# Prompt attention of a hybrid decoder step: high and low parts of the values side by side as one matmul's weights

## The chip, the cores and the metric

The kernel runs on one core of one Trainium2 chip. The metric is the device time of one launch in microseconds (us), lower is better; the time of a kernel is the median of its runs. The engines of a core are TensorE (PE, matrix products; its weight loads are shown as PEld), VectorE (DVE), ScalarE (ACT), GpSimd (POOL) and SyncE (SP), which issues most transfers. Each engine takes its instructions in the order in which the program holds them, and an instruction that waits holds up those behind it on its engine.

## The reference

One layer is applied to a prompt of 512 tokens and to 8 sample sequences of 8 new tokens with 2048 cached positions each. A latent attention and a convolution module share an input projection; their normalised outputs are concatenated and projected, and a gated feed-forward network with a short convolution follows. The change lies in the attention of the prompt, for which the reference computes (cut):

```python
def mla_attend(q_lat, q_rope, kv, q_pos, k_pos):
    ...
    s = jnp.einsum('bthc,bsc->bhts', q_lat, ckv) + jnp.einsum('bthr,bsr->bhts', q_rope, kr)
    ...
    p = jax.nn.softmax(s, axis=-1).astype(ckv.dtype)
    return jnp.einsum('bhts,bsc->bthc', p, ckv)
...
    attn = jnp.einsum('bthc,chv->bthv', o_lat, w_uv).reshape(b, t, D_ATT)
    mixed = jnp.concatenate([rmsnorm(attn, g_attn_out), rmsnorm(conv_y, g_conv_out)], axis=-1)
    x = x + mixed @ w_o
```

There are 8 heads (H) with values of 64 columns each (DV); everything is in fp32. The kernel forms for the prompt the values v = ckv · w_uv of all heads first (NP = 512 tokens as 4 blocks of 128) and multiplies the probabilities of a head with them.

## The kernel before

**Products of pairs.** TensorE works here on a rounded fp32 type. To keep the precision, an operand is held as a pair: `split` (L109 to L111) copies it rounded on ScalarE (the high part, L110) and subtracts that from the original on VectorE (the low part, L111). `mm3` (L122 to L125) multiplies two pairs in three matmuls: high by high (L123), high by low (L124), low by high (L125).

**Stages.** In the profiled execution the input projection and the convolution's input run to about 110 us; the decode stage, attention of the sample sequences over the cached pages with the convolution between it, to about 320 us; the prompt's attention from then to some 437 us, with the output projection of the convolution's half (`proj_conv`) laced in; then the rest of the output projection and, from about 460 us, the feed-forward network.

**Decode.** `load_chunk` fetches pages of the cache through SP's queue into the tiles `CR`. For a sequence `bt`, `rope_rows_of` (L599 to L602) copies the rotary columns of its four chunks `CR` to `RP` on ScalarE; `rope_keys` transposes `RP` on TensorE (bank `krb`). `keys` transposes a chunk (bank `ktb`) and splits it into `kh` and `kl`, and `scores` (L637 to L640) multiplies them with the queries (bank `sb`).

**Prompt attention.** `values_of(k)` computes the values of 128 tokens for all heads into a bank and splits them into `vh` and `vl`. These tiles hold, for each block k and pair of heads, three slots of 64 columns: first head, zeros, second head. `open_right` sets the zeros with eight memsets (L844, L845). A head then goes through

- `keys_of` for a pair of heads (bank `kb`), `head_in`: queries and keys split into `qT` and `kT`;
- `score(h, j)` for row blocks j = 0 to 3 (L970 to L973, bank `spb`, two of them): columns of 128 (j + 1); VectorE takes the maximum (L975), ScalarE the exponential into a buffer of the ring `Pm` (L977, three buffers);
- `prob`, `prob_T`: normalised, transposed by TensorE (bank `tb`) and split into the pair `PTp` (called `PT` in the code);
- `attend(h, k)` (L1001 to L1008), the value product: for k = 0 to 3 one `mm3` with 512 − 128 k columns into the bank `pv`. The weights of the first head of a pair are its 64 values and the 64 zeros, those of the second head the zeros and its values, so that both heads of a pair add into one bank of 128 rows;
- for each pair of heads `head_out` (copy `raw` of the bank, L1012; scaled and split into `atph` and `atpl`, L1013, L1014) and `head_ss` (transposes of `raw` by TensorE into the bank `rawb`, and their squares).

**What sets the order.** The program is written as generators in which the front of head h + 1 alternates with the back of head h. A scheduler places each instruction of an engine by a priority, the place in the program plus an offset from the table `PR` (L146), which `prio(key)` adds. The tiles' memory is planned by a pool; a tile that takes memory which another one used waits for that one's last reader. The keys in question are `rr` (`rope_rows_of`), `cn` and `l1` (parts of the convolution's normalisation), `r0`, `pn` (parts of decode) and `kT` (the key's rotary rows of the prompt).

## Time and profile before

| what | us |
|---|---|
| median of 3 runs | 895.66 |
| lowest and highest run | 895.3 and 901.98 |
| the profiled execution's own time | 892.08 |
| its span (first to last recorded instruction) | 890.3 |

The profiled execution is another one than the three timed runs. A row of the trace names start and duration, the engine, the line of the kernel (for `split`, `mm3` and transposes that of the helper), what is written from what, partitions by elements, and in brackets the idle time ahead of the instruction with what ended it. The duration of a matmul reaches into the next one, since they are pipelined; the distance between two starts is what a matmul costs in a row of them. PEclk or granted clock is the share of TensorE's full clock (2.4 GHz) that was granted; 0.50 is its lower level of 1.2 GHz.

### The profile page before, as it was taken

What the parts mean: (1) busy time and instruction counts of PE and PEld (TensorE: products, weight loads), DVE (VectorE), ACT (ScalarE), POOL (GpSimd) and SP (SyncE); (2) the same over time, 40 slices, a digit from 0 to 9 for tenths busy, and PEclk for the clock granted to TensorE, in tenths of its full rate; (3) what the DMA queues carried; (4) which work ended last, traced back from release to release, by engine and by line L of the source; (5) the groups of instructions that cost most, each with busy time, mean ns of one, the idle gap of its engine ahead of it and who ended that gap; (6) DMA issues with size and microseconds to landing.
All of it is one profiled execution on the core that took longest, in us unless ns stands there. A gap on an engine that the chain in (4) does not pass through costs nothing.

```text
span 890.3 us, 16024 instructions
## 1 busy us (share of the span) xinstructions
PE 850.3 (96%) x5724; PEld 756.0 (85%) x5724; DVE 652.4 (73%) x1159; ACT 452.6 (51%) x1028; POOL 310.8 (35%) x402
## 2 busy tenths in 40 slices
PE   6999998899989999999989999999999999999995
PEld 5999887577656767877769999999999999999994
DVE  5277449779998777777666777985677998689664
ACT  6224735777767887456444443444333443333353
POOL 3020499999991020000102121440011331078143
PEclk9999989989999999999999999999999999999998
DMA  6223153454333004010343222223322223422512
GB/s 220 93 63 100 40 166 86 130 151 129 93 107 84 24 25 154 24 49 27 116 141 126 93 79 87 72 73 95 119 76 91 72 72 95 142 72 61 196 37 107
DMA packets 53828, 84.33 MB, mean 95 GB/s; under 512 B 6066, under 2 KB 39795, under 8 KB 53748
## 3 DMA queue, kind: packets, MB, share of 16 engines
q1 hardware_dynamic: 53458, 82.75, 30.0%
q8 instruction: 45, 0.74, 0.4%
q10 hardware_dynamic: 290, 0.56, 0.2%
q14 instruction: 35, 0.29, 0.1%
HBM read 76.95 MB, written 6.34 MB: 94 GB/s over the span
## 4 chain that ended last, share of the span: by engine, by line
PE 85%; DVE 5%; ACT 3%; SPq 3%; issue 2%; DMA 1%; POOL 1%; POOLq 0%; DVEq 0%; ACTq 0%
PE ub L133 11%; PE ub L131 11%; PE ub L129 10%; PE db L125 3%; PE db L123 3%; PE db L124 3%; PE ob L703 3%; PE gb L133 2%; PE wob L123 2%; PE wob L125 2%; PE wob L124 2%; PE gb L129 2%; PE ktb L107 2%; PE gb L131 2%; PE pq L123 1%
## 5 line engine op out<-in xcount | busy, mean ns | idle before, releaser
L133 PE MATMUL ub<-h2h,wup_l 128*128 128x288 f32 x704 | 153.1, 294 | 0.6 <-DVE wup_l L111 0.6
L131 PE MATMUL ub<-h2l,wup_h 128*128 128x288 f32 x704 | 152.9, 295 | 0.0
L129 PE MATMUL ub<-h2h,wup_h 128*128 128x288 f32 x704 | 152.1, 293 | 0.0
L133 PEld LDWEIGHTS ub<-h2h,wup_l 128*128 128x128 f32 x704 | 113.4, 188 | 0.9 <-DVE wup_l L111 0.8
L129 PEld LDWEIGHTS ub<-h2h,wup_h 128*128 128x128 f32 x704 | 113.5, 188 | 0.1
L131 PEld LDWEIGHTS ub<-h2l,wup_h 128*128 128x128 f32 x704 | 113.0, 187 | 0.0
L111 DVE TENSOR_TENSOR wup_l<-wup_r,wup_h 128x1024 fp32r<-128x1024 f32 x44 | 56.3, 1278 | 50.7 <-ACT wup_h L110 50.7
L249 POOL TENSOR_TENSOR acc<-acc,ct 128x512 f32<-128x512 f32 x65 | 91.4, 1406 | 5.4
L110 ACT CAST wup_h<-wup_r 128x1024 fp32r<-128x1024 f32 x44 | 46.3, 1052 | 89.4 <-issue 48.2
L119 POOL TENSOR_TENSOR rstd<-ms,mhalf 128x1 f32<-128x1 f32 (+3 forms) x25 | 16.6, 671 | 214.5 <-ACT junk L1023 111.0
L1251 POOL COPY nf<-U 128x2 f32<-128x2 f32 x44 | 23.1, 526 | 122.0 <-ACT U L1249 122.0
L248 POOL TENSOR_SCALAR ct<-gx,vc 128x512 f32<-128x512 f32 x65 | 62.1, 956 | 6.0
L1247 POOL COPY U<-sfs 128x16 f32<-128x16 f32 x44 | 19.7, 453 | 98.4 <-DVE uo L1258 90.4
L111 DVE TENSOR_TENSOR kl<-ktb,kh 128x512 fp32r<-128x512 f32 x64 | 42.4, 682 | 8.0 <-ACT kh L110 7.6
L107 PE MATMUL ktb<-ident,CR 128*128 128x128 f32 x256 | 44.0, 285 | 0.6 <-DVE kl L111 0.5
L1258 DVE SCALAR_TENSOR_TENSOR uo<-U,vc,uo 128x592 f32<-128x592 f32 x44 | 39.3, 893 | 1.4
L1257 DVE SCALAR_TENSOR_TENSOR uo<-U,vc,uo 128x592 f32<-128x592 f32 x44 | 39.2, 892 | 1.0
L110 ACT CAST kh<-ktb 128x512 fp32r<-128x512 f32 x64 | 35.9, 588 | 7.6 <-PE ktb L107 4.3
L107 PEld LDWEIGHTS ktb<-ident,CR 128*128 128x128 f32 x256 | 30.8, 143 | 8.3 <-issue 4.6
L703 PE MATMUL ob<-CR,PF 128*64 128x256 f32 x128 | 36.8, 396 | 0.0
L1256 DVE TENSOR_SCALAR uo<-U,vc 128x592 f32<-128x592 f32 x44 | 31.3, 712 | 0.1
L637 PE MATMUL sb<-kh,QL 128*128 128x512 f32 x64 | 29.1, 454 | 2.4 <-DVE mx L644 1.8
(422 smaller groups left out, 2453.1 us busy)
## 6 DMA issues: line engine op xcount, KB each, us to landing
wup_r<-in_wup_dram SPq DMA_DIRECT2D x44, 512.0 KB, 3.5
CR<-in_cache_dram SPq DMA_DIRECT2D x128, 144.0 KB, 2.2
wdn_r<-in_wdn_dram SPq DMA_DIRECT2D x56, 128.0 KB, 2.5
x<-in_x_dram SPq DMA_DIRECT2D x8, 512.0 KB, 4.6
wg_r<-in_wglu_dram SPq DMA_DIRECT2D x8, 512.0 KB, 3.2
wo_r<-in_wo_dram SPq DMA_DIRECT2D x8, 512.0 KB, 3.4
wdn_r<-in_wdn_dram SPq DMA_DIRECT2D x8, 384.0 KB, 3.1
x2d<-x SPq DMA_DIRECT2D x4, 512.0 KB, 2.7
```

The costliest lines, as they stand in the source:

```text
L107: T.transpose(out, in_, ident[:n, :n])
L110: last["hi"] = A.copy(hi, src).ins
L111: last["split"] = V.tensor_tensor(lo, src, f(hi), ALU.subtract).ins
L123: T.matmul(out, lh, rh, start=start, stop=False)
L124: T.matmul(out, lh, rl, start=False, stop=False)
L125: T.matmul(out, ll, rh, start=False, stop=stop)
L129: T.matmul(o, lh, rh, start=start, stop=False)
L131: T.matmul(o, lh, rl, start=False, stop=False)
L133: T.matmul(o, ll, rh, start=False, stop=stop)
L248: G.tensor_scalar(t, xm, w, 1.0, ALU.mult, ALU.mult)
L249: G.tensor_tensor(am, am, t, ALU.add)
L703: T.matmul(o[:NS, :DC], PF[:, j % 2, k], CRS[4 * bt + j][:, k, :DC], start=False, stop=False)
```

## The change

High and low parts of the values lie side by side in one tile `vv`, four slots of 64 columns for a pair of heads: high of the first, low of the first, low of the second, high of the second. The weights of a matmul of `attend` are the high and the low part of one head (128 columns), so that one matmul multiplies both with the high part of the probabilities and a second one both with the low part: two matmuls for each k in place of three. The product of low and low, left out before, is contained. The result of a head is then the sum of two halves of the bank's rows: the new function `head_sum` copies one half on ScalarE and adds the other on VectorE, for each head. A bank now belongs to one head, where two heads of a pair shared it. The tile `raw` is filled by the two heads' sums; it comes from the ring `Pm`, which has four buffers now, and is held from the first head's sum to the second head's `head_ss`. The copy of 128x512 in `head_out` goes, and the memsets go. Six numbers of the table `PR` change: `cn` −76 to −116, `l1` 42 to −100, `rr` 80 to −100, `pn` 45 to 50, `r0` 38 to 65, `kT` 15 to 14.

```diff
@@ -143,7 +143,7 @@
         return hi, lo
 
 
-    PR = dict(ux=20, ul=-150, dw0=0, dw1=0, fm=0, uc=0, pl=300, dj=-37, p0=-119, pr=-37, fs=-95, expo=95, wv=110, ft=-45, f0=-600, v2=574, av=-135, cs0=600, cv=300, vs=90, cn=-76, att=-85, cs1=600, l4=20, q0=300, later=100, h2=35, l1=42, sq0=-45, lo=-360, wk=180, vb=19, lT=-594, v0=35, gl2=37, wo=-540, g0=-300, rq=-30, cso=600, gl1=-40, sc1=25, rr=80, keys=-32, k0=600, pn=45, fs0=-30, ho=-45, pj=-5, l0=-15, f7=32, q4=120, r0=38, sc0=5, kT=15, aT=-300, rk=-12, sq1=19)
+    PR = dict(ux=20, ul=-150, dw0=0, dw1=0, fm=0, uc=0, pl=300, dj=-37, p0=-119, pr=-37, fs=-95, expo=95, wv=110, ft=-45, f0=-600, v2=574, av=-135, cs0=600, cv=300, vs=90, cn=-116, att=-85, cs1=600, l4=20, q0=300, later=100, h2=35, l1=-100, sq0=-45, lo=-360, wk=180, vb=19, lT=-594, v0=35, gl2=37, wo=-540, g0=-300, rq=-30, cso=600, gl1=-40, sc1=25, rr=-100, keys=-32, k0=600, pn=50, fs0=-30, ho=-45, pj=-5, l0=-15, f7=32, q4=120, r0=65, sc0=5, kT=14, aT=-300, rk=-12, sq1=19)
 
     class prio:
         def __init__(self, key):
@@ -838,14 +838,11 @@
         kx.close()
         pr = R["pr"] = R.setdefault("prx", ExitStack()).enter_context(
             tc.tile_pool(name="pr", bufs=2, reuse_waits="tile"))
-        R["vh"] = pr.tile([P, 4, 4, 3, DV], F32R, name="vh", bufs=1)
-        R["vl"] = pr.tile([P, 4, 4, 3, DV], F32R, name="vl", bufs=1)
-        for k in range(4):
-            G.memset(f(R["vh"][:, k, :, 1]), 0.0)
-            G.memset(f(R["vl"][:, k, :, 1]), 0.0)
+
+        R["vv"] = pr.tile([P, 4, 4, 4, DV], F32R, name="vv", bufs=1)
         R["kT"] = [pr.tile([96, 2, NP], F32R, name=f"kT{i}", bufs=1) for i in range(2)]
         R["wk"] = pr.tile([P, 2, 1024], F32R, name="wk", bufs=1)
-        touch(pr, ("qT", [96, 2, NP], F32R, 2), ("Pm", [P, 512], F32, 3))
+        touch(pr, ("qT", [96, 2, NP], F32R, 2), ("Pm", [P, 512], F32, 4))
         R["wkr"] = pr.tile([P, 1024], F32, name="wkr", tag="qT")
         nc.sync.dma_start(R["wkr"], wuk)
 
@@ -880,7 +877,7 @@
             mm3(b, ckvh[:, ct, k * P:(k + 1) * P], ckvl[:, ct, k * P:(k + 1) * P], wv[:, 0, sl], wv[:, 1, sl],
                 ct == 0, ct == 1)
         bv = b.rearrange("p (q s d) -> p q s d", q=4, s=2)
-        split(R["vh"][:, k, :, 0:3:2], R["vl"][:, k, :, 0:3:2], bv)
+        split(R["vv"][:, k, :, 0:4:3], R["vv"][:, k, :, 1:3], bv)
 
     def conv_scaled(m):
         cvh, cvl = R["cv"]
@@ -973,7 +970,7 @@
         T.matmul(s[:, j * P:n], identb, cmask, start=False, stop=True)
         nm = small("nm")
         V.tensor_reduce(nm[:, 0:1], s[:, :n], AX.X, ALU.max, negate=True)
-        Pm = R["pr"].tile([P, 512], F32, name="Pm", tag="Pm", bufs=3)
+        Pm = R["pr"].tile([P, 512], F32, name="Pm", tag="Pm", bufs=4)
         A.activation(Pm[:, :n], s[:, :n], AF.Exp, bias=nm[:, 0:1], accum_out=nm[:, 1:2])
         hs["P", h, j] = Pm, nm
 
@@ -999,20 +996,28 @@
         split(dst[0], dst[1], tb[:, :n].rearrange("p (k q) -> p k q", q=P))
 
     def attend(h, k):
+
         hh, p_ = h % 2, h // 2
-        if hh == 0 and k == 0:
-            hs["pv"] = bank("pv", "o")
-        pv, PT = hs["pv"], hs["PT", h]
-        a, l = (R[v][:, k, p_].rearrange("p s d -> p (s d)")[:, hh * DV:hh * DV + P] for v in ("vh", "vl"))
+        if k == 0:
+            hs["pv", h] = bank("pv", "o")
+        pv, PT = hs["pv", h], hs["PT", h]
+        v = R["vv"][:, k, p_, 2 * hh:2 * hh + 2].rearrange("p s d -> p (s d)")
         c = slice(384 * k + k * P, 384 * k + NP)
-        mm3(pv[:, k * P:], a, l, PT[:, 0, c], PT[:, 1, c], hh == 0 and k == 0, hh == 1 and k == 3)
+        T.matmul(pv[:, k * P:], v, PT[:, 0, c], start=k == 0, stop=False)
+        T.matmul(pv[:, k * P:], v, PT[:, 1, c], start=False, stop=k == 3)
+
+    def head_sum(h):
+        if h % 2 == 0:
+            hs["raw"] = R["pr"].tile([P, 512], F32, name="raw", tag="Pm", bufs=4)
+        own, other = slice(h % 2 * DV, h % 2 * DV + DV), slice(DV - h % 2 * DV, P - h % 2 * DV)
+        raw, pv = hs["raw"], hs.pop(("pv", h))
+        A.copy(raw[own], pv[other])
+        V.tensor_tensor(raw[own], pv[own], raw[own], ALU.add)
 
     def head_out(p_):
-        raw = R["pr"].tile([P, 512], F32, name="raw", tag="Pm", bufs=3)
-        A.copy(raw, hs["pv"])
+        raw = hs["raw"]
         A.activation(R["atp"][0][:, p_], raw, AF.Copy, scale=vcol("gao", p_))
         V.scalar_tensor_tensor(R["atp"][1][:, p_], raw, vcol("gao", p_), f(R["atp"][0][:, p_]), ALU.mult, ALU.subtract)
-        hs["raw"] = raw
 
     def head_ss(p_):
         b = bank("rawb", "k")
@@ -1121,6 +1126,8 @@
             with prio("att"):
                 attend(h, k)
             yield
+        with prio("ho"):
+            head_sum(h)
         if h % 2:
             with prio("ho"):
                 head_out(h // 2)
```

On TensorE, at the value product of head 6 (`pv`; `wob` is the output product of the convolution's half, `tb` the transposes of the next head's probabilities), the kernel before has:

```order
L972 MATMUL spb<-kT_4958,qT 128x512
L973 LDWEIGHTS identb
L973 MATMUL spb<-cmask,identb 128x128
L123 MATMUL pv<-PTp,vh 128x512
L107 MATMUL tb<-ident,Pm 128x128
L123 MATMUL wob<-wo_h,atph 128x512
L124 MATMUL pv<-PTp,vh 128x512
L125 MATMUL pv<-PTp,vl 128x512
L123 MATMUL pv<-PTp,vh 128x384
```

The changed kernel has there:

```order
L969 MATMUL spb<-kT_4949,qT 128x512
L1006 MATMUL pv<-PTp,vv 128x512
L970 LDWEIGHTS identb
L970 MATMUL spb<-cmask,identb 128x128
L1007 MATMUL pv<-PTp,vv 128x512
L1006 MATMUL pv<-PTp,vv 128x384
L1007 MATMUL pv<-PTp,vv 128x384
L1006 MATMUL pv<-PTp,vv 128x256
L1007 MATMUL pv<-PTp,vv 128x256
L1006 MATMUL pv<-PTp,vv 128x128
L1007 MATMUL pv<-PTp,vv 128x128
L107 MATMUL tb<-ident,Pm 128x128 x2
```

The output product `wob` and the transpose stood between the first and the second matmul of the value product, and stand behind the last one now.

On ScalarE, at the start of the prompt's attention (`Pm` are exponentials, `cvh` the convolution's scaled output, `PTp` the high part of the transposed probabilities, `wo_h` of the output weights), the kernel before has:

```order
L977 ACTIVATE Pm,nm<-spb,nm 128x512
L110 CAST PTp<-tb 128x128
L887 ACTIVATE cvh<-acc,vc 128x576
L977 ACTIVATE Pm,nm<-spb,nm 128x128
L110 CAST PTp<-tb 128x2x128
L110 CAST PTp<-tb 128x3x128
L110 CAST wo_h<-wo_r 128x1024
L887 ACTIVATE cvh<-acc,vc 128x576
L977 ACTIVATE Pm,nm<-spb,nm 128x256
```

The changed kernel has there:

```order
L974 ACTIVATE Pm,nm<-spb,nm 128x512
L974 ACTIVATE Pm,nm<-spb,nm 128x128
L110 CAST PTp<-tb 128x128
L884 ACTIVATE cvh<-acc,vc 128x576
L110 CAST PTp<-tb 128x2x128
L884 ACTIVATE cvh<-acc,vc 128x576
L974 ACTIVATE Pm,nm<-spb,nm 128x256
L110 CAST wo_h<-wo_r 128x1024
L110 CAST PTp<-tb 128x3x128
```

Head 1's first exponential (128x128) moved ahead of a cast and of a piece of `cvh`, and its second (128x256) ahead of the weight's cast.

On ScalarE in the decode stage, at the rotary copies of the third sequence (`kh` are keys, `sl` and `ch` other copies of that stage), the difference is:

```order
 L643 COPY sl<-sb 64x512 x2
 L689 CAST ch<-CR 128x512
-L110 CAST kh<-ktb 128x512
-L602 COPY RP<-CR 128x4x32
+L602 COPY RP<-CR 128x4x32
+L110 CAST kh<-ktb 128x512
 L614 CAST QZ_858<-QR 32x128
 L110 CAST kh<-ktb 128x512
```

The copy from `CR` to `RP`, which needs a page of the cache, stands ahead of a key cast now, behind which it stood before.

## Rows read from the trace of the kernel before

**Rows 1.** The page's head and part 1: the span, then busy time, share of the span and number of instructions of each engine.

```profile
span 890.3 us, 16024 instructions
PE 850.3 (96%) x5724; PEld 756.0 (85%) x5724; DVE 652.4 (73%) x1159; ACT 452.6 (51%) x1028; POOL 310.8 (35%) x402
```

**Rows 2.** Busy time of each engine in stretches of the span; columns: stretch, its length, PE, PEld, DVE, ACT and POOL busy with the number of instructions, granted clock, share of the DMA engines, GB/s.

```profile
136.00:316.00 180.00, 166.56 (x1013) 119.92 (x1011) 154.33 (x317) 130.56 (x281) 127.37 (x109) 0.98 0.37 102
350.00:400.00 50.00, 49.84 (x288) 39.93 (x287) 38.26 (x89) 28.38 (x81) 0.00 (x0) 1.00 0.16 53
400.00:437.00 37.00, 33.58 (x185) 26.56 (x184) 26.29 (x66) 21.37 (x60) 1.00 (x2) 1.00 0.17 58
```

**Rows 3.** What TensorE waited for, from 350 to 400 us (first row), and its two main waits from 400 to 437 us: us in total, times, longest.

```profile
PE spb L970 <- ACT Pm L977: 0.2, 1, 0.2
...
PE wob L123 <- ACT Pm L977: 1.0, 1, 1.0
...
PE pv L123 <- ACT PTp L110: 0.7, 1, 0.7
```

**Rows 4.** The timeline of TensorE in the value product of head 0: each third matmul (L125) and the matmul behind it; columns: start, us, engine, line, operation, out<-in, tile.

```profile
352.58 0.39 PE L125 MATMUL pv<-PTp,vl 128*128 128x512 f32 x1
352.81 0.33 PE L123 MATMUL pv<-PTp,vh 128*128 128x384 f32 x1
...
353.16 0.34 PE L125 MATMUL pv<-PTp,vl 128*128 128x384 f32 x1
353.33 0.28 PE L123 MATMUL pv<-PTp,vh 128*128 128x256 f32 x1
...
353.57 0.27 PE L125 MATMUL pv<-PTp,vl 128*128 128x256 f32 x1
353.68 0.22 PE L123 MATMUL pv<-PTp,vh 128*128 128x128 f32 x1
...
353.85 0.28 PE L125 MATMUL pv<-PTp,vl 128*128 128x128 f32 x1
353.97 0.29 PE L107 MATMUL tb<-ident,Pm 128*128 128x128 f32 x1
```

**Rows 5.** The third matmuls, the casts and subtractions of the keys, and four of the eight memsets, grouped by tile and form: number, shortest/mean/longest ns, first and last start; sizes.

```profile
L125 PE MATMUL pv<-PTp,vl x32: 272/308/477, 352.6 to 433.0; 128*128 128x512 f32 x8, 128*128 128x384 f32 x8, 128*128 128x256 f32 x8, 128*128 128x128 f32 x8
...
L110 ACT CAST kT<-kb x8: 578/582/586, 331.8 to 409.4; 64x512 fp32r<-64x512 f32 x8
L111 DVE TENSOR_TENSOR kT<-kb,kT x8: 682/688/694, 332.4 to 410.0; 64x512 fp32r<-64x512 f32 x8
...
L844 POOL MEMSET vh<- x4: 308/310/312, 317.7 to 319.2; 128x256 f32 x4
```

**Rows 6.** The timeline around head 6's value product, its last matmul, and the first value matmul of head 7.

```profile
422.81 0.68 DVE L111 TENSOR_TENSOR PTp<-tb,PTp 128x512 fp32r<-128x512 f32 x1
...
423.65 0.50 PE L123 MATMUL wob<-wo_h,atph 128*128 128x512 f32 x1 [1.02 <-ACT Pm L977]
423.99 0.39 PE L124 MATMUL pv<-PTp,vh 128*128 128x512 f32 x1
...
425.50 0.28 PE L125 MATMUL pv<-PTp,vl 128*128 128x128 f32 x1
...
430.71 0.49 PE L123 MATMUL pv<-PTp,vh 128*128 128x512 f32 x1 [0.68 <-ACT PTp L110]
```

**Rows 7.** The timeline at the end of head 7's value product: a weight's split on VectorE, the copy of the pair, the transposes of that copy.

```profile
431.70 1.23 DVE L111 TENSOR_TENSOR wo_l<-wo_r,wo_h 128x1024 fp32r<-128x1024 f32 x1 [0.32 <-ACT wo_h L110]
...
433.36 0.59 ACT L1012 COPY raw<-pv 128x512 f32<-128x512 f32 x1 [1.69 <-PE pv L125]
...
434.00 0.66 PE L107 MATMUL rawb<-ident,raw 128*128 128x128 f32 x4
```

**Rows 8.** The timeline of TensorE at the start of the prompt's attention.

```profile
345.45 0.39 PE L970 MATMUL spb<-kT,qT 96*128 96x256 f32 x1 [1.89 <-ACT Pm L977]
```

**Rows 9.** What ScalarE waited for in the decode stage (110 to 320 us) at the rotary copies, and from the timeline a key cast, the rotary copy behind it and the scores that the cast feeds; the transposes of another sequence's rotary rows.

```profile
ACT RP L602 <- DMA CR<-in_cache_dram: 14.5, 10, 3.5
...
167.55 0.58 ACT L110 CAST kh<-ktb 128x512 fp32r<-128x512 f32 x1
...
170.56 0.30 ACT L602 COPY RP<-CR 128x128 f32<-128x128 f32 x1 [2.42 <-DMA CR<-in_cache_dram]
...
173.20 0.50 PE L637 MATMUL sb<-kh,QL 128*128 128x512 f32 x1
...
178.98 1.12 PE L107 MATMUL krb<-ident,RP 128*128 128x128 f32 x4 [2.04 <-ACT RP L602]
```

**Rows 10.** Busy time of each engine and the granted clock in stretches of 2 us behind two waits of TensorE; columns as in rows 2.

```profile
178.00:180.00 2.00, 1.02 (x6) 1.02 (x7) 2.00 (x4) 1.33 (x4) 2.00 (x2) 0.67 0.81 248
180.00:182.00 2.00, 2.00 (x15) 2.00 (x14) 1.31 (x2) 1.58 (x5) 1.82 (x3) 0.50 0.47 135
182.00:184.00 2.00, 2.00 (x7) 1.69 (x6) 1.59 (x6) 1.10 (x4) 1.83 (x2) 0.50 0.59 192
184.00:186.00 2.00, 2.00 (x10) 1.55 (x8) 0.85 (x2) 0.83 (x2) 1.90 (x2) 0.63 0.71 199
...
346.00:348.00 2.00, 2.00 (x11) 1.63 (x9) 2.00 (x7) 1.55 (x6) 0.00 (x0) 0.50 0.00 0
348.00:350.00 2.00, 2.00 (x10) 1.83 (x10) 1.74 (x5) 2.00 (x5) 0.00 (x0) 0.67 0.00 0
```

## The prediction

> **What bounds the kernel now.** I read the page's busy line first: TensorE's matmuls cover 850.3 of the span's 890.3 us and VectorE's work 73% [rows 1]. So time goes when TensorE gets fewer or cheaper matmuls, or idles less, and everything else only matters where TensorE waits for it. Next the windows by stage, since the change touches two stages. In the decode stage (136 to 316 us) TensorE is busy for 166.56 of 180 us, so some 13.4 us of waiting lie there; in the middle of the prompt attention (350 to 400 us) it is busy for 49.84 of 50 us; in its last two heads (400 to 437 us) for 33.58 of 37 us [rows 2]. The waits agree: between 350 and 400 us TensorE waited once, for 0.2 us; between 400 and 437 us the longest is 1.0 us, an output product behind ScalarE's exponential, and the next 0.7 us, the last head's value product behind its transposed probabilities [rows 3]. The reader is to see that in heads 0 to 5 a matmul that goes is time that goes, and that in heads 6 and 7 it may only turn into waiting.
>
> **The third pass that goes.** A head's value product has four blocks of 512, 384, 256 and 128 columns with three matmuls each; the third goes. Its price is not its duration in the trace (matmuls overlap) but the distance from its start to the next matmul's start. For the four third matmuls of head 0 these are 352.81 − 352.58 = 0.23, 353.33 − 353.16 = 0.17, 353.68 − 353.57 = 0.11 and 353.97 − 353.85 = 0.12 us, 0.63 us in all [rows 4]. There are 32 of them, one a block for each of eight heads [rows 5]. Heads 0 to 5 lie where TensorE does not wait: 6 × 0.63 = −3.8 us. The Trainium skill, page "TensorE: Matmul & The Clock Gate", section "Back-to-back issue gap", says that in a sustained stream of weight load and matmul the two set the spacing together, and gives about 81 ns at 128 columns and 131 ns at 512. Between them by a straight line a head's third pass would be 81 + 98 + 114 + 131 = 424 ns, an estimate, six heads would give 2.5 us and the sum below would end 1.3 us higher. The trace has 0.12 and 0.23 us for the same widths in this kernel's 4-byte type, so it does not agree, and the trace is what I use.
>
> **Head 6.** Here the place in the order counts. Before, TensorE started the head's first value matmul, then stood 1.02 us at the output product, which waited for an exponential, started that at 423.65 and the second value matmul at 423.99; the value product ended at 425.78 [rows 6]. Now that output product stands behind the whole value product, so the wait falls on the second value matmul, which needs the low half of the probabilities: VectorE writes it until 422.81 + 0.68 = 423.49 [rows 6]. The remaining seven matmuls take 0.23 + 2 × (0.17 + 0.11 + 0.12) = 1.03 us, to 424.5; then comes the output product with its 0.34 us, which ended up ahead before. So the same work is done by 424.9 in place of 425.8, less the transposes moved in between: −0.7 us, between −0.6 and −0.9.
>
> **Head 7.** Value product and normalisation are a chain now. Before: ScalarE's copy of the pair (128x512) at 433.36 for 0.59 us, then the transposes that need it at 434.00 [rows 7]. Now the product ends 0.6 us earlier, about 432.7, but then ScalarE copies 64x512 and VectorE adds 64x512. Neither operation is in the trace; the nearest rows are the casts of 64x512 from PSUM into the keys (0.58 us) and their subtractions with one operand in PSUM (0.69 us) [rows 5]. So 432.7 + 0.6 + 0.7 = 434.0; VectorE's split ahead of it ends at 431.70 + 1.23 = 432.93, in time [rows 7]. Head 7 gives 0: the pass saved pays for the sum. If the add were as long as the split, +0.5.
>
> **The other seven sums.** They add 8 × 0.69 = 5.5 us to VectorE, and to ScalarE 8 × 0.58 in place of the four pair copies of 0.59, +2.3 us. Over some 85 us that lifts VectorE from 38.26/50 = 77% to 83% and ScalarE from 57% to 60% [rows 2]. What hides them is TensorE's work between two heads' value products: the next product may not start until the bank is read, and the shortest such gap is head 6 to 7, from 425.50 + 0.28 = 425.8 to 430.71, 4.9 us for a sum of 1.3 us [rows 6]. I take 0. Without that cover a head costs the sum's 1.3 us less the pass saved, so 7 × 0.65 = +4.5 at the very worst; engines that are 83% busy and run their queues in order could make it late in one or two places, so the bound that I keep is +1.5. Pm's ring grows by the buffer that the half-finished sum now holds, so exponentials have three as before: 0. The eight memsets of 0.31 us on GpSimd go; nothing waits there: 0 [rows 5].
>
> **The start of attention.** Head 1's last scores now stand before the first output product and the next keys. They need a score bank that ScalarE frees, and there TensorE already waited 1.89 us for an exponential [rows 8]. Head 1's first exponential now stands ahead of two other activations, its second is no longer behind a weight cast, so the release may come in time; the bounds are 0 and +1, I take +0.5.
>
> **The table.** Four of its keys move decode and convolution work by a few rows. The copies of the rotary part of the cached pages are moved ahead of a key cast or two. All such copies waited 14.5 us for pages, in ten pieces. Example: the copy at 170.56 stood 2.42 us for its page; the cast that ended before it (167.55 + 0.58) is now behind it, so it ends near 171.5, while the scores that it feeds began at 173.20 [rows 9]. Cost 0, but only by 1.7 us. Elsewhere the copy's own delay did stop TensorE: 2.04 us at 178.98 [rows 9]. No row says by how much the pages will be later or sooner; the bounds are the two rivals below, and I take 0 since the moved casts have this slack and TensorE's order in this stage hardly changes.
>
> **The sum.** −3.8 − 0.7 + 0 + 0.5 = −4.0 us, against the profiled execution's 892.08 that is 888.1. That execution lies 3.6 us below the median of the runs, 895.66, so on the scale of the medians 891.7 us. Its own range: −2 (start +1, sums late +1.5) to −7 (start 0, waits of the decode stage shrink by some 2), that is 888.7 to 893.7.
>
> **Rivals.** First, **the gain is eaten**: VectorE and ScalarE reach the sums late, or the waits of heads 6 and 7 take it all. For it: VectorE at 83% and a ring of one bank; against it: gaps of 4.9 us and more. Price: 0, 893.7 to 897.5.
>
> Second, **slower: a rope copy holds ScalarE in front of a key cast whose scores TensorE needs**. Place: one of the moved copies; the page isn't there, ScalarE stands, casts and scores follow late. It decides when TensorE stands about 2 us at one place, because then the clock follows: after the 2.04 us wait at 178.98 the granted clock was 0.67, 0.50, 0.50 and 0.63 in four windows of 2 us [rows 9, 10], which is the lower of the two levels (1.2 GHz against 2.4) for most of them, and loses 0.66 + 1.0 + 1.0 + 0.74 = 3.4 us. With the wait that is 5.4 us for one such place: 895.66 − 4.0 + 5.4 = 897.1; two give 902.5. For it: ten waits, the longest 3.5 us; against it: the slack of 1.7 us in the example. The Trainium skill, the same page, part 1 on the clock gate, says that the clock is set by how busy TensorE has been recently; this trace agrees at 179 and 346 us.
>
> Third, **faster: such a place goes**. If the copy at 179 us comes in time, 2.0 + 3.4 = 5.4 us come back: 886.3. If the wait at 345.45 shrinks too, its 1.9 us and the half clock behind it, 0.50 and 0.67 in two windows (1.0 + 0.66 = 1.7 us) [rows 8, 10]: 882.7. For it: the copies do stand earlier now; against it: the copy at 179 waited for the page, not for its place in the order, and pages don't come sooner.
>
> **How the numbers follow.** Forecast 0.60; gain eaten 0.14; a new wait with half clock 0.08 once and 0.04 twice; one such place gone 0.06, both 0.04; 0.04 for other effects of the reordering, of either sign. Predicted 891.7. The range 886.0 to 898.0 holds the forecast, the eaten gain, and either clock case once, and leaves out some 0.12. One per cent, about what a measurement of this kernel can tell, is 9 us: faster means under 886.7. Faster: 0.10 (the clock cases with one or both places gone). Slower, over 904.6: 0.04, only with two or more new waits. Same: 0.86.
>
> **What would show it.** The third pass: 64 value matmuls in place of 96, distances as before, the stretch from the first to the last value product 4 us shorter. The sums: TensorE's waits at the first value matmul of a head for the previous sum, near 0. Head 6: the output product no longer waits. Head 7: the transposes wait for the add, and start about 1.3 us after the last value matmul. The table: waits of the rope copies and the windows of half clock near 179 and 346 us; if either moves, the size is wrong by 3 to 5 us although the pass is priced right. Wrong altogether would be a value product whose matmuls no longer follow at 0.12 to 0.23 us.

## The result and the profile after

The changed kernel takes 901.08 us in the median of 20 runs (898.82 to 904.59), the kernel before 895.47 us in 20 runs of the same kind (891.51 to 901.98). The ratio is 1.007, with a 95% interval of 1.0052 to 1.0088: some 6 us slower. 891.7 us with a range of 886.0 to 898.0 was predicted. The profiled execution of the changed kernel took 901.33 us, 9.3 us more than that of before; 3.4 us of this is that the traced execution of before lay under its median, so the two traces alone show too much.

The page of the changed kernel, its head and part 1, answers to [rows 1]:

```profile
span 899.6 us, 15956 instructions
PE 854.1 (95%) x5692; PEld 756.1 (84%) x5692; DVE 655.8 (73%) x1167; ACT 456.7 (51%) x1032; POOL 304.4 (34%) x394
```

TensorE has 32 matmuls fewer and is busy for 3.8 us longer. The busy time by stretch shows where (columns as in [rows 2]; the stretches are decode as there, then from head 0's value product to head 7's queries, then the last two heads):

```profile
136.00:316.00 180.00, 164.67 (x997) 119.13 (x996) 150.07 (x311) 128.57 (x274) 122.13 (x107) 0.98 0.36 102
356.30:419.00 62.70, 61.44 (x345) 47.98 (x344) 51.62 (x116) 38.77 (x104) 0.00 (x0) 1.00 0.11 34
419.00:443.00 24.00, 20.11 (x79) 14.60 (x78) 14.91 (x34) 11.93 (x35) 0.00 (x0) 0.72 0.23 81
```

The granted clock is 0.72 in the last stretch, where before it was 1.00 [rows 2]. Two-us and four-us stretches of the changed kernel, first at the start of attention, then in the last heads, answer to [rows 10]:

```profile
348.00:350.00 2.00, 1.25 (x6) 1.15 (x7) 1.51 (x8) 2.00 (x8) 0.00 (x0) 0.50 0.00 0
350.00:352.00 2.00, 2.00 (x10) 1.70 (x10) 0.76 (x2) 2.00 (x5) 0.00 (x0) 0.50 0.00 0
352.00:354.00 2.00, 2.00 (x9) 1.48 (x7) 1.80 (x4) 1.65 (x4) 0.00 (x0) 0.50 0.00 0
354.00:356.00 2.00, 2.00 (x9) 1.58 (x9) 2.00 (x4) 0.31 (x1) 0.00 (x0) 0.81 0.00 0
...
420.00:422.00 2.00, 1.39 (x9) 1.06 (x10) 1.90 (x7) 1.55 (x10) 0.00 (x0) 1.00 0.68 203
422.00:424.00 2.00, 1.67 (x10) 1.25 (x9) 1.65 (x6) 1.58 (x4) 0.00 (x0) 0.75 0.15 59
424.00:428.00 4.00, 3.70 (x11) 2.39 (x11) 3.19 (x7) 1.30 (x5) 0.00 (x0) 0.50 0.09 19
428.00:432.00 4.00, 3.08 (x12) 2.49 (x11) 2.09 (x8) 2.54 (x6) 0.00 (x0) 0.50 0.29 112
432.00:436.00 4.00, 4.00 (x12) 3.11 (x12) 1.66 (x3) 0.94 (x3) 0.00 (x0) 0.50 0.23 82
436.00:438.00 2.00, 1.98 (x10) 1.37 (x8) 0.56 (x1) 0.13 (x1) 0.00 (x0) 0.83 0.24 98
```

TensorE ran at its lower level of 1.2 GHz from about 423.0 to 436.6 us, 13.6 us; in the kernel before there is no such stretch here. At the start of attention the stretch is 6.8 us long (348.0 to 354.8) where before it was 3.4 (346.0 to 349.4). The timeline of TensorE ahead of and in the long stretch:

```profile
419.90 0.33 PE L967 MATMUL spb<-kT,qT 96*128 96x128 f32 x1 [0.40 <-ACT qT L110]
...
420.76 0.33 PE L969 MATMUL spb<-kT,qT 96*128 96x128 f32 x1 [0.42 <-DVE qT L111]
...
421.34 0.39 PE L967 MATMUL spb<-kT,qT 96*128 96x256 f32 x1 [0.19 <-ACT Pm L974]
...
423.31 0.69 PE L967 MATMUL spb<-kT,qT 96*128 96x384 f32 x1 [0.33 <-ACT Pm L974]
...
430.77 0.79 PE L123 MATMUL wob<-wo_h,atph 128*128 128x512 f32 x1 [0.92 <-ACT Pm L974]
...
442.03 0.65 PE L107 MATMUL rawb<-ident,raw 128*128 128x128 f32 x4 [0.43 <-DVE raw L1015]
```

The scores of head 7 (the rows from 419.90 to 423.31) wait for queries, then for the low part of the queries, then for exponentials, each time for 0.2 to 0.4 us. The clock falls between the third and the fourth of these rows. In the kernel before the waits at the same place were 0.57, 0.24 and 0.64 us, and the clock stayed; its timeline there:

```profile
417.35 0.33 PE L970 MATMUL spb<-kT,qT 96*128 96x128 f32 x1 [0.57 <-ACT qT L110]
...
418.02 0.38 PE L970 MATMUL spb<-kT,qT 96*128 96x256 f32 x1 [0.24 <-ACT Pm L977]
...
420.54 0.44 PE L970 MATMUL spb<-kT,qT 96*128 96x384 f32 x1 [0.64 <-ACT Pm L977]
```

In the changed kernel the output product at 430.77 waits 0.92 us, about as before (1.02) [rows 6], and the transposes of `rawb` at 442.03 wait 0.43 us for VectorE's addition, where before they followed the copy [rows 7].

The exponentials of head 7's third and fourth scores, for which that output product waits, come late. VectorE has the maximum of the third scores (128x384) ready at 424.81 + 0.56 = 425.37 us. But ScalarE has the copy of head 6's sum ahead of the exponential in its order, and stands 4.13 us until head 6's value product has ended; the exponential starts at 430.04, 4.67 us behind its maximum. The kernel before has no copy at this place, and the exponential starts 0.03 us behind the maximum. First the changed kernel, then the kernel before:

```profile
424.81 0.56 DVE L972 TENSOR_REDUCE nm<-spb 128x1 f32<-128x384 f32 x1 [0.93 <-PE spb L970]
...
429.43 0.58 ACT L1014 COPY raw<-pv 64x512 f32<-64x512 f32 x1 [4.13 <-PE pv L1007]
...
430.04 0.58 ACT L974 ACTIVATE Pm<-spb,nm 128x384 f32<-128x384 f32 x1
...
422.35 0.55 DVE L975 TENSOR_REDUCE nm<-spb 128x1 f32<-128x384 f32 x1
...
422.93 0.58 ACT L977 ACTIVATE Pm<-spb,nm 128x384 f32<-128x384 f32 x1
```

This is so in every trace. In the ten of kernels with a copy for each head (the changed kernel twice, e1, e5, e6, e9, e10, e11, e13, e14, explained below) the exponential stands behind the copy and starts 3.2 to 7.4 us after its maximum, whether the clock fell or not. In the six without (before, e2, e3, e7, e8, e12) it starts 0.03 or 0.04 us after.

The pass itself went as priced. Head 0 of the changed kernel, TensorE's timeline:

```profile
357.82 0.39 PE L1007 MATMUL pv<-PTp,vv 128*128 128x512 f32 x1
358.05 0.34 PE L1006 MATMUL pv<-PTp,vv 128*128 128x384 f32 x1
358.23 0.34 PE L1007 MATMUL pv<-PTp,vv 128*128 128x384 f32 x1
358.41 0.28 PE L1006 MATMUL pv<-PTp,vv 128*128 128x256 f32 x1
```

The distances are 0.23, 0.18 and 0.18 us, as in [rows 4]. The prices taken for the sums hold as well; the copies and additions by tile:

```profile
L1014 ACT COPY raw<-pv x8: 578/580/585, 359.0 to 440.7; 64x512 f32<-64x512 f32 x8
L1015 DVE TENSOR_TENSOR raw<-pv,raw x8: 673/689/695, 360.5 to 441.3; 64x512 f32<-64x512 f32 x8
```

**Where the time went.** The program is cut at starts of matmuls of the timeline: the last product of the query latents (`qlb`), the last of the sample's values (`avb`), the last query transposes (`qtb`, head 7), the last value product (`pv`), the first up-projection (`ub`) and the last output transposes (`yb`). The table gives the lengths between them in us, for the two traced kernels and one trace of each experiment (labels e1 to e14, explained below), and in the last two columns how long the clock was at its lower level around the start of attention and in the last heads (granted clock in stretches of 0.2 us).

| kernel | decode: qlb to avb | avb to qtb | last heads: qtb to pv | pv to ub | ub to yb | lower clock at start | in last heads |
|---|---|---|---|---|---|---|---|
| before | 217.1 | 74.1 | 17.2 | 31.1 | 412.5 | 3.4 | 0 |
| changed | 219.2 | 73.5 | 21.8 | 31.8 | 413.7 | 6.8 | 13.6 |
| changed, second trace (e4) | 221.2 | 73.5 | 21.8 | 31.8 | 413.3 | 6.8 | 13.6 |
| e1 code, old table | 216.7 | 72.0 | 21.9 | 31.8 | 413.4 | 3.4 | 13.6 |
| e2 table only | 219.5 | 75.4 | 17.2 | 31.1 | 412.4 | 6.8 | 0 |
| e3 two passes, no sums | 218.5 | 71.7 | 16.1 | 32.0 | 414.3 | 3.4 | 0 |
| e5 six matmuls | 217.2 | 71.6 | 19.7 | 31.8 | 413.4 | 3.4 | 3.4 |
| e6 six and eight | 218.0 | 70.5 | 18.9 | 31.9 | 413.2 | 0 | 0 |
| e7 rr only | 221.1 | 75.2 | 17.2 | 31.1 | 412.6 | 6.8 | 0 |
| e8 table without rr | 218.4 | 75.1 | 17.4 | 31.1 | 412.5 | 6.8 | 0 |
| e9 scores ahead | 218.7 | 73.0 | 22.4 | 31.8 | 414.1 | 6.8 | 13.6 |
| e10 four and eight, ahead | 219.8 | 70.8 | 23.0 | 31.8 | 412.5 | 0 | 13.6 |
| e11 changed, six and eight | 219.6 | 70.7 | 19.0 | 31.8 | 412.9 | 0 | 0 |
| e12 before with eight | 220.1 | 73.7 | 17.3 | 31.1 | 412.4 | 0 | 0 |
| e13 no additions | 217.1 | 72.1 | 18.9 | 31.6 | 414.0 | 3.4 | 3.4 |
| e14 six and eight, ahead | 219.8 | 70.6 | 19.4 | 31.8 | 412.5 | 0 | 0 |

Between the traces of before and changed, the last heads have 4.6 us of the loss, decode 2.1, the rest 0.7 and 1.2; the stretch that holds the passes of heads 0 to 5 gains 0.6. Another 1.2 us lie ahead of the table's first cut.

### The profile page after: what moved, and what is told of

It reads as the page before. It is cut to its first block, busy times and chain, and to the rows that moved or that the text cites. A ratio compares the mean times of both kernels' runs of the same rounds, so it can differ in the third digit from the quotient of the medians.

```text
span 899.6 us, 15956 instructions
## 1 busy us (share of the span) xinstructions
PE 854.1 (95%) x5692; PEld 756.1 (84%) x5692; DVE 655.8 (73%) x1167; ACT 456.7 (51%) x1032; POOL 304.4 (34%) x394
## 4 chain that ended last, share of the span: by engine, by line
PE 75%; DVE 8%; ACT 5%; SPq 4%; issue 4%; DMA 2%; POOL 1%; DVEq 0%; POOLq 0%; ACTq 0%
PE ub L133 10%; PE ub L131 10%; PE ub L129 10%; PE db L125 3%; PE db L123 2%; PE db L124 2%; PE gb L133 2%; PE gb L129 2%; PE gb L131 2%; SPq L594 2%; PE wob L123 2%; PE wob L124 2%; SPq L595 2%; PE wob L125 2%; PE ob L703 2%
## 5 line engine op out<-in xcount | busy, mean ns | idle before, releaser
L248 POOL TENSOR_SCALAR ct<-gx,vc 128x512 f32<-128x512 f32 x65 | 60.3, 928 | 6.0
L110 ACT CAST kh<-ktb 128x512 fp32r<-128x512 f32 x64 | 35.9, 588 | 10.1 <-PE ktb L107 6.8
L107 PEld LDWEIGHTS ktb<-ident,CR 128*128 128x128 f32 x256 | 31.6, 145 | 9.6 <-issue 4.2
```

The lines of the kernel that those rows point to most:

```text
L107: T.transpose(out, in_, ident[:n, :n])
L110: last["hi"] = A.copy(hi, src).ins
L248: G.tensor_scalar(t, xm, w, 1.0, ALU.mult, ALU.mult)
```

## The experiments

Each was timed against the kernel before on the same chip in five rounds; ratios are to before, with the 95% interval. Where instructions are added or left out, the scheduler also moves others: in e3, e5, e6 and e9 to e14 some scores, masks, transposes, casts or output products of the prompt's attention stand in other places than in the kernel they are built on, so none of these changes one thing alone.

**Code and table apart.** The changed kernel holds two changes that can be taken one at a time. With the old table the order of decode is that of before; with the new table alone the order of the prompt's attention on TensorE is that of before.

```diff
 e1, on the changed kernel:
-cn=-116, l1=-100, rr=-100, pn=50, r0=65, kT=14
+cn=-76, l1=42, rr=80, pn=45, r0=38, kT=15
 e2, on the kernel before:
-cn=-76, l1=42, rr=80, pn=45, r0=38, kT=15
+cn=-116, l1=-100, rr=-100, pn=50, r0=65, kT=14
```

> The changed code with the table of the kernel before: decode is ordered as before, only the prompt's attention is changed. Theory A (the loss is in the attention itself: in the changed kernel's trace the last value matmul lay 7.3 us later than before and the decode's end 3.3 us later, so the attention lost 4 to 5 us by a clock that fell to half at 423 us, and stayed there to 436.5): slower than before by 3 to 5 us, with half clock in the last two heads. Theory B (the loss comes from the table; the fall at 423 us follows from where the decode ends): about 4 us faster than before, as predicted for the code, without half clock in the last two heads.

> The kernel before with the changed kernel's table: three passes, pair copy and memsets as before, only decode and convolution reordered. Theory A: slower by 2 to 4 us, the 3.3 us that the changed kernel was late at the end of decode, no half clock in heads 6 and 7. Theory B: slower by 8 to 10 us, with half clock in the attention's last heads too.

e1 took 896.63 us, 1.0028 (1.0006 to 1.0051); e2 897.36 us, 1.0035 (1.0013 to 1.0057). The two nearly add up to the changed kernel's 1.007 (1.0063): each part is slower by some 2.5 to 3 us. e2 is within theory A's 2 to 4 us, e1 a little under its 3 to 5. Theory B, by which the code alone would be 4 us faster, fell: e1's clock falls in the last heads too. Its granted clock there, columns as before:

```profile
414.00:416.00 2.00, 1.40 (x11) 1.02 (x10) 1.90 (x7) 1.35 (x8) 0.00 (x0) 1.00 0.77 240
416.00:418.00 2.00, 1.68 (x9) 1.24 (x7) 1.46 (x6) 1.78 (x5) 0.00 (x0) 0.76 0.06 23
...
424.00:428.00 4.00, 3.44 (x8) 2.77 (x9) 3.33 (x7) 2.38 (x6) 0.00 (x0) 0.50 0.00 0
```

e2 has full clock in the last heads, and shows the longer stretch at the start of attention, although TensorE's order there is that of before:

```profile
348.00:350.00 2.00, 0.85 (x4) 0.85 (x5) 1.67 (x9) 1.93 (x6) 0.00 (x0) 0.58 0.00 0
350.00:352.00 2.00, 2.00 (x10) 1.72 (x9) 1.90 (x6) 1.35 (x5) 0.00 (x0) 0.50 0.00 0
352.00:354.00 2.00, 2.00 (x9) 1.72 (x9) 1.61 (x3) 2.00 (x5) 0.00 (x0) 0.50 0.00 0
```

**The pass alone.** e3 is the kernel before without the third matmul; the product of the values' low part is left out, and there are no sums.

```diff
-        mm3(pv[:, k * P:], a, l, PT[:, 0, c], PT[:, 1, c], hh == 0 and k == 0, hh == 1 and k == 3)
+        T.matmul(pv[:, k * P:], a, PT[:, 0, c], start=hh == 0 and k == 0, stop=False)
+        T.matmul(pv[:, k * P:], a, PT[:, 1, c], start=False, stop=hh == 1 and k == 3)
```

> The kernel before without the third matmul of each value product (the low part of the values is left out of the result), everything else as it was, no sums. It prices the pass. Theory A1 (TensorE has less to do in heads 6 and 7, so its waits weigh more and the clock falls there whatever the sums do): half clock behind 420 us, time from -1 to +3 us against before. Theory A2 (the waits that the sums and their order bring make the clock fall): full clock there, 4 to 5 us faster than before.

891.77 us, 0.9959 (0.9937 to 0.9981): 3.7 us faster by the ratio. The clock stays up in the last heads:

```profile
416.00:420.00 4.00, 2.94 (x24) 2.32 (x22) 3.83 (x11) 3.74 (x16) 0.00 (x0) 1.00 0.41 131
420.00:434.00 14.00, 11.03 (x57) 8.04 (x55) 9.48 (x22) 8.55 (x19) 0.00 (x0) 1.00 0.27 82
```

So A1 fell: fewer matmuls alone don't bring the clock down. Yet this is no proof that waits do: TensorE is busy here for 2.94 of 4 us at head 7's start, and in the changed kernel, from 418 to 422 us, for 1.60 + 1.39 = 2.99 of 4. By waiting alone the two can't be told apart. By the table the pass gives 2.4 us from `avb` to `qtb` and 1.1 us in the last heads; some of it is lost again behind the last value product (0.9 and 1.8 us).

**The changed kernel again.**

> The changed kernel once more, for its second trace. If its loss is systematic: half clock from about 423 to 436 us again, near 254 us and 348 to 354 us again, 901 us. If the fall of the clock comes and goes from one execution to the next: other places, and times that scatter by the 3 to 7 us that such a stretch costs.

901.5 us (10 runs), 1.0066 (1.004 to 1.0092). The lower clock came back in the last heads (427.6 to 441.2, again 13.6 us), at the start of attention (6.8 us) and near 257 us. It is systematic at these places; the third is taken up under the table's keys. Nor do the traces alone say so: the mean granted clock of a run has its median at 0.982 in the kernel before (126 runs) and at 0.9745 in the changed kernel (20 runs). Over a span of some 899 us the difference is 0.0075 × 2 × 899 = 13.5 us more at the lower level, an estimate, and about the 13.6 us of the traces.

**Filling the waits.** Six matmuls of 128x512 that nobody reads were put at head 7's start, and in e6 eight more at the start of attention (six of them in the wait of 1.9 us [rows 8]). They write the bank that the next value product overwrites; that product takes this bank in place of a new one (an edit of `attend`, not shown).

```diff
 e5, on e1, behind the transposes of raw of heads 4 and 5 (head_ss):
+        if p_ == 2:
+            pv = hs["pv", 6] = bank("pv", "o")
+            for i in range(6):
+                T.matmul(pv, R["wk"][:, 0, :P], R["wk"][:, 0, :512], start=True, stop=True)
 e6, also behind head 1's queries (head_front):
+        if h == 1:
+            pv = hs["pv", 0] = bank("pv", "o")
+            for i in range(8):
+                T.matmul(pv, R["wk"][:, 0, :P], R["wk"][:, 0, :512], start=True, stop=True)
```

> The changed code with the old table, and six matmuls of 128x512 more, whose result is overwritten, between the transposes of head 7's queries and its second scores, into the bank of head 6's value product; they stand where TensorE waits 0.4, 0.4 and 0.2 us. Theory C (the clock falls because TensorE is thin from the last transposes to head 7's scores): no half clock in the last heads, about 6 us faster than the same kernel without them, 890 to 891 us. Rival D (the fall has another cause, or the value product's new order brings it): half clock again, 897 to 898 us, the 1.4 us of work added.

> As the kernel with the six matmuls at head 7, with eight more at the start of attention, six of them in the wait of 1.9 us ahead of head 1's second scores, after which the clock was at its lower level for 3.4 us in the traces with the old table. Theory C: that stretch of half clock goes too, 1.5 to 2 us faster than with the six alone, about 889 us. Rival D: no change or 0.5 us slower by the two matmuls that stand ahead of other work.

e5 took 896.09 us, 1.0 (0.9978 to 1.0023); e6 895.34 us, 0.999 (0.9969 to 1.0011). In e6 the clock stays up at both places, as theory C said (start of attention, then the last heads):

```profile
346.00:348.00 2.00, 1.88 (x10) 1.27 (x9) 1.79 (x7) 2.00 (x8) 0.00 (x0) 1.00 0.00 0
348.00:350.00 2.00, 1.62 (x12) 1.48 (x12) 1.57 (x8) 2.00 (x8) 0.00 (x0) 1.00 0.00 0
...
417.00:419.00 2.00, 2.00 (x14) 1.67 (x15) 1.83 (x6) 2.00 (x11) 0.00 (x0) 1.00 0.38 150
419.00:423.00 4.00, 2.74 (x16) 1.92 (x15) 4.00 (x11) 2.35 (x7) 0.00 (x0) 1.00 0.24 66
423.00:427.00 4.00, 1.58 (x12) 1.28 (x10) 2.88 (x7) 2.71 (x7) 0.00 (x0) 1.00 0.16 66
```

The Trainium skill, page "TensorE: Matmul & The Clock Gate", part 1 on the clock gate, says that the clock follows how busy TensorE has been; here e1's code with more work for TensorE in its waits keeps 1.00 where e1 has 0.50, so the trace agrees. The filling can't be told apart from the new order that comes with it. In time theory C was too hopeful: e6 is some 3 us faster than e1 by the ratios (their intervals touch), e5 and e1 can't be told apart, and 6 us were expected from e5 alone. In e5 the clock still fell once, from 421.0 to 424.4. And at full clock the last heads are not short either (18.9 us in e6, of which the six matmuls added are 1.4 at the distance of 0.23 us). TensorE's waits in e6, 414 to 440 us:

```profile
PE wob L123 <- ACT Pm L974: 2.5, 1, 2.5
PE rawb L107 <- DVE raw L1015: 1.4, 1, 1.4
```

The output product now waits 2.5 us for head 7's exponential, and VectorE is busy for all 4.00 us from 419 to 423. On ScalarE a weight cast that waits 2.27 us for its weights and the copy of head 6's sum stand ahead of that exponential, which starts 3.2 us after its maximum. So the trace puts part of what the clock gives back into waiting for an exponential behind the copy.

e11 is the changed kernel with its own table and the same matmuls as e6.

> The changed kernel with its own table, and the six and eight matmuls. If half clock in the attention is what its code loses: 3 to 5 us faster than the changed kernel, what is left over before is the table's 2 to 3 us in decode. If not: 901 to 902 us as the changed kernel, or slower by the matmuls added.

897.45 us, 1.0023 (1.0001 to 1.0044), as expected: 1.007 − 1.0023 is some 4 us. The clock stays up at both places, 73.5 and 21.8 us become 70.7 and 19.0. What is left over before is about what the table costs in e2.

e12 is the kernel before with the eight matmuls at the start.

> The kernel before with eight matmuls of 128x512 at the start of attention alone, six in its wait of 1.9 us. If the 3.4 us of half clock behind that wait cost what the clock's loss says (1.7 us): 1 to 1.7 us faster than before. If what follows is bound by ScalarE anyway: within 0.5 us of before.

895.58 us, 1.0006 (0.998 to 1.0033). The 3.4 us of lower clock went, and the time did not move by more than can be told; from `avb` to `qtb` the trace has 73.7 in place of 74.1 us. This short stretch cost little.

**Order or clock.** e9 puts head 7's four scores ahead of head 6's value product; e10 does that with four matmuls in head 7's waits and the eight at the start, e14 with six and eight.

```diff
 on e1 (e9), on e6 with four in place of six (e10) and on e6 (e14), in head_front:
                 with prio("fs"):
+                    tc.cur_priority -= 60 * (h == 7)
                     score(h, j)
                     prob(h, j)
+                    tc.cur_priority += 60 * (h == 7)
```

> The changed code with the old table; only head 7's scores get a priority 60 higher, so that all four stand ahead of head 6's value product and of some transposes. Nothing is added. Theory C (TensorE's thin stretch at head 7's start makes the clock fall, and the waits there are the same): half clock in the last heads again, within 1.5 us of the kernel without this. Theory G (the scores' and masks' place behind transposes and value product makes the last heads late): 2 to 4 us faster than the changed code with the old table.

> The changed code with the old table, head 7's scores ahead as in the kernel before this, four matmuls of 128x512 in head 7's waits and eight at the start of attention. If the clock and the late scores each take a part of what the pass gave: no half clock from 340 us on, the distance from the last decode product to the last value product 4 to 5 us shorter than before, the time 2 to 4 us under before. If the last heads are bound by a chain through VectorE and ScalarE whatever the clock is: as the kernel with six and eight matmuls, about the time of before.

> The changed code with the old table, eight matmuls at the start of attention, six in head 7's waits, and head 7's scores 60 ahead. With six matmuls the clock stayed up, with four and the scores ahead it fell; if the six keep it up here too and the scores' place costs what their late mask suggests (1 us): 1 to 3 us faster than before, the last part under 18.9 us. If the clock falls with the scores ahead whatever fills: about the time of before, the last part 22 us.

e9: 898.52 us, 1.0039 (1.0018 to 1.006); theory G fell, the scores ahead gain nothing, and the clock falls again. Their exponentials stay behind the copy of head 6's sum: that of the third scores starts 7.4 us after its maximum in e9, 6.3 in e10 and 4.7 in e14. e10: 894.24 us, 0.9994 (0.9971 to 1.0016); in its trace the clock falls in spite of four matmuls. That trace need not stand for the other runs of e10: its execution took 896.88 us at a mean clock of 0.978, and their medians are 894.24 us and 0.981. In 417 to 419 us, ahead of the fall, TensorE is busy for half the time:

```profile
417.00:419.00 2.00, 1.00 (x7) 0.72 (x8) 1.58 (x5) 1.75 (x6) 0.00 (x0) 1.00 0.00 0
419.00:421.00 2.00, 2.00 (x7) 1.31 (x6) 1.68 (x6) 0.55 (x3) 0.00 (x0) 0.51 0.25 29
```

e14: 895.97 us, 1.0009 (0.999 to 1.0028); full clock, and still 19.4 us in the last heads. Neither expectation of the two kernels was met in full: with the clock up and the scores early the last heads take as long as in e6. None of these versions beats the kernel before by more than the measurement can tell.

**The additions.** e13 is e1 without VectorE's additions; the half of a head's result that lies on its own rows is left out.

```diff
-        V.tensor_tensor(raw[own], pv[own], raw[own], ALU.add)
```

> The changed code with the old table, without VectorE's additions (the half of a head's result that lies on its own rows is left out); copies, matmuls and their number stay. Theory J (the additions make VectorE late at head 7's start and so let the clock fall): full clock in the last heads, the last value product 16 to 17 us behind head 7's query transposes as in the kernel with two passes and no sums, 4 to 6 us faster than with the additions. Theory K (order and number of TensorE's matmuls decide it): half clock again, some 22 us there.

894.95 us, 1.0001 (0.9983 to 1.0019), some 2.4 us faster than e1 by the ratios (the intervals overlap), less than the 4 to 6 of theory J. At head 7's start the clock stays up, though TensorE's order there is that of e1 (VectorE and ScalarE have some instructions in other places); the copy stays, and the third exponential starts 4.0 us after its maximum. Later, behind a wait of 1.1 us for transposed probabilities and one of 1.1 us for an exponential, it falls for 3.4 us:

```profile
414.00:416.00 2.00, 1.59 (x11) 1.24 (x11) 1.82 (x7) 1.57 (x10) 0.00 (x0) 1.00 0.48 182
416.00:418.00 2.00, 1.67 (x11) 1.19 (x10) 1.52 (x7) 1.82 (x6) 0.00 (x0) 1.00 0.20 80
...
422.00:424.00 2.00, 0.87 (x3) 0.70 (x3) 0.72 (x3) 1.98 (x6) 0.00 (x0) 0.75 0.40 162
424.00:426.00 2.00, 2.00 (x7) 1.51 (x6) 1.72 (x4) 1.03 (x2) 0.00 (x0) 0.50 0.00 0
```

K, that order and number of the matmuls alone decide it, does not fit this trace; J fits it in the clock at head 7's start, in one trace of one kernel, and is too large in time.

**The table's keys.** e7 changes `rr` alone on the kernel before, e8 the five other keys.

```diff
 e7:
-rr=80
+rr=-100
 e8:
-cn=-76, l1=42, pn=45, r0=38, kT=15
+cn=-116, l1=-100, pn=50, r0=65, kT=14
```

> The kernel before with only the rotary copies' key rr changed, 80 to -100. Theory E (ScalarE held by a copy whose page is not there costs decode the 2 us by which the whole table made it longer): 1.5 to 3 us slower than before, most of what the whole table cost. Theory F (the convolution's and the other keys cost it): within 1 us of before.

> The kernel before with the five other keys of the table changed, cn, l1, pn, r0 and kT, and rr as it was. Theory E: within 1 us of before, the stretch of half clock at the start of attention 3.4 us long as before. Theory F: 1.5 to 3 us slower.

e7: 896.58 us, 1.0006 (0.9981 to 1.0032); e8: 898.0 us, 1.0025 (0.9996 to 1.0054). E, that `rr` brings the loss, is not borne out by the times, though e7's decode is among the longest of the traces, 221.1 us; F can't be called shown, since both intervals hold no change. Each of the two has the longer stretch of lower clock at the start of attention, so neither group of keys is its only cause. In sum the copies' waits for pages grew little: 14.5 us in 10 before [rows 9], 14.4 us in 11 in e2, 16.7 us in 11 in the changed kernel.

At one place, though, `rr` does much what the prediction's second rival describes. In the kernel before a copy stands behind two exponentials of the decode stage (`S`) and finds its page there (first row). In the changed kernel it stands ahead of them and a key cast, waits 2.44 us for its page, and TensorE waits 2.33 us for the exponential (second and third row):

```profile
251.14 0.29 ACT L602 COPY RP<-CR 128x128 f32<-128x128 f32 x1
...
251.57 0.30 ACT L602 COPY RP<-CR 128x128 f32<-128x128 f32 x1 [2.44 <-DMA CR<-in_cache_dram]
...
254.28 0.71 PE L107 MATMUL ptb<-ident,S 64*128 64x64 f32 x8 [2.33 <-ACT S L659]
```

Behind it the clock is at its lower level for 3.4 us (255.8 to 259.2). All five traces of kernels with the new `rr` (the changed kernel twice, e2, e7, e11) have this wait, of 2.1 to 3.0 us, with 3.4 or 6.8 us of lower clock behind it; none of the eleven others has it. Their decode takes 220.1 us on the mean (219.2 to 221.2) and that of the others 218.3 (216.7 to 220.1). The ranges overlap, and e7's time shows no loss, so that the place is shown and its price is not.

## Why the prediction was wrong

**The third pass: right, slightly too large.** Distances and prices hold. From the first value product to head 7's query transposes (351.01 to 415.85 us in the trace before) 64.8 us became 62.2 in the changed kernel, 2.6 less, and 61.4 in e3, 3.4 less, where 3.8 was predicted for heads 0 to 5. The additions are hardly what is missing: e1 takes 61.9 us there, and e13, without them, 62.0.

**Heads 6 and 7: the step that failed.** The sum had −0.7 and 0 there; the traces of the changed code have +4.6 to +4.7 us, with 13.6 us of lower clock. Two things were left out. The first is the order on ScalarE. The change puts a copy for head 6 there, where the kernel before had none; it waits for the whole value product (4.13 us), and head 7's exponentials stand behind it. They start 11.5 us behind head 7's query transposes, where before it was 7.1. The sign that was named for head 6, that the output product no longer waits, did not come for this reason: it waits 0.92 us for such an exponential. The second is the clock. The rival of a new wait with half clock had the right mechanism and, for this place, the wrong condition. It was looked for at rotary copies in decode, where it also came true, near 254 us, and was to decide only when TensorE stood for about 2 us at one place. Here no wait ahead of the fall was longer than 0.42 us, and the fall lasted twice as long as the stretch at 179 us on which the price was based. That the cost is the clock's in part is borne out by e6 and e11, which keep the clock with work that nobody needs: 21.9 and 21.8 us become 18.9 and 19.0. That the rest is the copy ahead of the exponentials is read from the traces; no experiment puts the copy behind them, so it is not shown by one. That the additions have a part in the fall is borne out by e13 alone.

**The other seven sums.** 0 was taken because TensorE's work between two value products, 4.9 us and more, is longer than a sum. That covers the bank that the sum reads. It does not cover what stands behind the copy on ScalarE while the copy waits for the value product. In heads 0 to 5 TensorE stayed busy all the same (61.44 of 62.70 us); in the last heads it did not (20.11 of 24.00 us, part of it at half clock), and VectorE is full there (3.90 of 4 us from 418 to 422).

**The start of attention: mis-sized.** +0.5 was taken, 0 to +1 the bounds. From `avb` to the first value product the traces have 9.3 us before and 11.3 in the changed kernel, +2.0: the code alone (e1) +0.8, the table alone (e2) +1.2, the latter with the lower clock for 6.8 us in place of 3.4. But e3, e5, e7, e8 and e13 have 10.1 to 10.3 there as well, so that some 0.8 us of each may be that the one trace of before is short.

**The table: the sum's 0 was wrong, its cause is not settled.** Alone it costs 1.0035, some 3 us, and two more pairs agree: the changed kernel against e1 (1.007 and 1.0028) and e11 against e6 (1.0023 and 0.999). The runs do not show more time at the lower clock for it: the median of their mean clocks is 0.982 in e2 as before. The traces put it into decode and the start of attention. But decode scatters: seven traces of kernels with the old table and an unchanged decode order (before, e1, e3, e5, e6, e9, e13) lie between 216.7 and 218.7 us, and three more (e10, e12, e14) at 219.8 and 220.1, as high as the new table's 219.2 to 221.2. So one trace of each says little about 2 us there. The sum's reason for 0, that a moved copy has slack, holds for its example and not for the copy near 251 us.

**Faster by a vanished half clock: wrong in price.** Between 131 and 340 us e5 has no lower clock at all, before had it for 6.8 us at 179, and decode took 217.2 and 217.1 us. e5 still waits 1.52 us for that copy. In these two traces the lower clock does not show in the stage's length, so the 5.4 us that this rival was to give back were not to be had, and the slower rival's price at that place may be too high for the same reason.

**Head 7's end and behind it.** From the last value product to the first up-projection every kernel with two passes takes 0.5 to 0.9 us more than the 31.1 of before, e3 without sums too. So the pass saved in head 7 ends its product earlier and nothing else: the 0 for head 7 fits, but not only because of the sum. The network itself, taken as 0, is up to 1.8 us longer in most of these traces.

**Sum against the medians.** Code +2.5 us (e1) where −4.0 was predicted, table +3.1 us (e2) where 0 was. The pass alone is worth 3.7 us (e3), so the code's sums, order and clock cost some 6. The low end of the sum's own range, −7, comes to −6.5 by its terms (−3.8 − 0.7 − 2).

What stays open: why the clock falls at head 7's start in the changed code and not in the kernel before or in e3, whose TensorE is busy for about the same share there (3.05 and 2.94 of 4 us from 416 to 420); what the copy ahead of head 7's exponentials costs by itself; and which keys of the table cost its 3 us. For the second a kernel with that copy behind the exponentials would be needed, for the others a trace for each of several executions.

## What to carry to other kernels

Work that is taken from the busiest engine is worth its price only while that engine stays the limit. Where it shares the limit with others, as in the last heads here, the time saved can turn into waits. An instruction that the change adds to another engine has two prices: its own length, and what stands behind it in that engine's order while it waits for its input. The first was worked out here (0.58 us), the second was not (4.13 us). So before trusting a sum, go through the stretches where the busiest engine already waits a little, and ask what the change adds to the engine it waits for, and ahead of what. And a stretch at half clock need not cost its full loss: compare the stage's length with and without it.

## What the runs showed of the hardware

Matmuls of work that nobody reads, six at one place and eight at another, went with a granted clock of 1.00 where it was otherwise 0.50 for 13.6 and 3.4 us, at no loss in time (e6 against e1: 0.999 and 1.0028). The clock fell behind waits of only 0.2 to 0.4 us in a stretch in which TensorE was busy for 2.99 of 4 us, while the kernel before kept it behind waits of 0.57, 0.24 and 0.64 us.

A lower clock for 6.8 us in decode cost nothing that the stage's length shows in two traces (217.1 against 217.2 us). Over many runs the two go together: in the 126 runs of the kernel before, a mean granted clock that is 0.01 lower goes with a time that is 4.6 us longer (correlation −0.77; clocks 0.970 to 0.988, times 890.4 to 901.3 us). Had TensorE been the limit throughout, 0.01 would be about 8.9 us, an estimate (0.01 × 893). This is a correlation alone: the waits ahead of a fall cost time too.
